# Feed-forward weight blocks in divided units: the first sum of each unit made by an accumulating transfer instead of VectorE

## The chip, the cores and the metric

The kernel runs on one core of one Trainium2 chip. A core has TensorE (PE, matrix products into PSUM), VectorE (DVE), ScalarE (ACT), GpSimd (POOL) and SyncE (SP), each with a queue of its own that it works through in order, and 16 DMA engines that all queues share. The metric is device time in microseconds (us), the median of several executions.

## What is computed

One inference step of a small hybrid decoder layer for 1048 tokens (16 meta tokens, 1024 prompt tokens, 8 single-token samples), model width 1024, in float32:

```python
def swiglu(x, wg, wu, wd):
    return (jax.nn.silu(x @ wg) * (x @ wu)) @ wd

def decoder_layer(h, ...):
    h = h + 0.5 * swiglu(rmsnorm(h, n1), w1g, w1u, w1d)
    u = rmsnorm(h, nm) @ w_in
    ...
    h = h + mix
    h = h + 0.5 * swiglu(rmsnorm(h, n2), w2g, w2u, w2d)
    return h, s_hg, s_ssm, conv_buf
```

Between the two feed-forward blocks lie two scans (an HGRN2 group and a Mamba-2 group) and an output projection. The change touches the two feed-forward blocks alone, and in them the products of the normed tokens with `wg` and `wu`. Hidden width is 2816, that is 22 columns of 128.

## The kernel before

**Products in three parts.** A float32 operand is split into a high and a low half in a faster format; a product is then three matmuls (high x high, high x low, low x high; lines 169 to 171). For a block of weights the high half is a cast on ScalarE (`hi`, line 497) and the low half a subtraction on VectorE (`lo`, line 501).

**Seven products for eight.** For one column of 128 hidden features, gate and up weights are cut along the model width into four blocks of 512 x 128, each stored on chip as 128 x 512. They are named by number: 1 (gate, first half), 7 (up, first half), 4 (up, second half) and 2 (gate, second half). A scheme of the Strassen kind replaces the eight block products with seven, at the price of sums of weight blocks, made in `Left.sum_`:

- 5 = 7 + 4
- 6 = 5 - 1
- 7 = 1 - 7, written over block 7
- 3 = 2 - 6

One column handled like this is a unit, a `Left` object. The sums are VectorE instructions over 128 x 512 (line 493).

**Divided units.** In each of the two feed-forward blocks the last 18 of the 22 columns are handled two at a time by `two_pairs`: product 3 of the two units is not done for each, but divided once more into seven smaller products for both together. These are the 18 divided units of a block, 36 in all. A pair of units takes 24 steps; a step is one product of 12 matmuls, in some steps with a smaller one behind it.

**What sets the order.** In the feed-forward blocks the queues of PE, VectorE, ScalarE and SP are written out by hand. `Steps` holds the PE steps; `S.before(i, fn)` puts a piece of other work ahead of step `i` in the program, and each engine's queue receives its instructions in that order. For a divided unit that begins at step `s0`, `plan_apart` (line 517) places loads at -10 to -7 (`load`, line 487, on SP's queue), sums at -5 to -2, and the split of each block 4 and 3 steps ahead of its product. POOL's queue is not written by hand; the scheduler places its instructions by what they depend on.

**Buffers.** Loaded blocks and sums lie in a ring of eight buffers of 128 x 512 (`raw`, tile name `r`). A load into a buffer waits on SP's queue until the buffer's last reader is done, and what stands behind it on SP waits too: also the stores of finished hidden blocks (line 994, `hd<-s`).

Of the kernel before, what the change touches and what calls it, by code (L numbers as in the profile page):

```python
# [13 lines left out]
ALU = mybir.AluOpType  # L14
# [3 lines left out]
P = 128  # L18
# [324 lines left out]
class Blocks:  # L343
# [19 lines left out]
    def sum_(self, p):  # L363
        x, y = {5: (7, 1), 6: (3, 5), 7: (3, 7), 4: (2, 6)}[p]
        x, y = self.b[x], self.b[y]
        t = self.b[p] if p == 7 else self.new(p)
        self.K.nc.vector.tensor_sub(t, x, y)  # L367
# [108 lines left out]
class Left:  # L476
# [8 lines left out]
    def load(self, p):  # L485
        self.raw[p] = self.K.raw(self.n * P)
        self.K.nc.sync.dma_start(self.raw[p].rearrange("p (k c) -> p k c", k=self.n), self.srcs[p])

    def sum_(self, p):
        x, y, op = {5: (7, 4, ALU.add), 6: (5, 1, ALU.subtract), 7: (1, 7, ALU.subtract), 3: (2, 6, ALU.subtract)}[p]  # L490
        if p not in self.raw:
            self.raw[p] = (self.K.t if p in self.apart else self.K.raw)(self.n * P)
        self.K.nc.vector.tensor_tensor(self.raw[p], self.raw[x], self.raw[y], op)  # L493
# [23 lines left out]
    def plan_apart(self, S, s0, uses):  # L517
        for p, d in ((7, -10), (4, -9), (1, -9), (2, -7)):
            S.before(s0 + d, lambda p=p: self.load(p))
        for p, d in ((5, -5), (6, -4), (7, -3), (3, -2)):  # L520
            S.before(s0 + d, lambda p=p: self.sum_(p))
        for p, d in uses.items():
            S.before(s0 + d - 4, lambda p=p: self.hi(p))
            S.before(s0 + d - 3, lambda p=p: self.lo(p))
# [515 lines left out]
def down(K, S, wdv, hidden, src, h, after):  # L1040
# [25 lines left out]
    def pieces(p, j, g, b, tag, late=0):  # L1066
# [33 lines left out]
        if p in (5, 6, 7, 3):  # L1100
            x, y = {5: (21, 22), 6: (0, 11), 7: (22, 0), 3: (12, 0)}[p]
            S.before(b - 9, lambda: sum_(x, y, ALU.add if p == 5 else ALU.subtract))
# [1465 lines left out]
```

## Time and profile before

| | us |
|---|---|
| median of 3 runs | 1922.8 (1922.28 to 1923.09) |
| the profiled execution | 1922.67 |
| its span | 1920.9 |

The profile is one execution seen by the hardware profiler. Its times count from the start of the span. Busy time of an engine is given in us, with the number of instructions in brackets where a window is shown; a row of a timeline has start, duration, engine, line, operation, output and inputs with the buffer numbers left out, and in square brackets the idle time before it and what ended it. A row for SP (SPq) is the issue of a transfer, not the transfer: what moves is seen in the last two columns of a window, the mean busy share of the 16 DMA engines and GB/s.

### The profile page before, as it was taken

The page shows a single profiled execution, that of the slowest core. Times are in us where ns is not written, and L with a number is a line of the kernel's source. Part 1 is how long each engine was busy: PE and PEld are TensorE (multiplying, and loading weights), DVE is VectorE, ACT ScalarE, POOL GpSimd, SP SyncE. Part 2 cuts the span into 40 slices and gives each one's busy share as a digit, 9 for nine tenths or more (in the row PEclk, how much of TensorE's full clock was granted, in tenths as well). Part 3 has the DMA queues.
Part 4 walks back from the last instruction along what each step waited for, and adds up shares of the span by engine and source line. Part 5 has one row for each costly group of instructions (what it writes and reads, how often), then busy time and mean ns, then how long its engine had stood idle before and what let it go on. Part 6 is the DMA issues. An engine that isn't in the chain of part 4 may idle for free.

```text
span 1920.9 us, 41195 instructions
## 1 busy us (share of the span) xinstructions
PE 1905.5 (99%) x16692; PEld 1875.2 (98%) x16692; DVE 1526.5 (79%) x2866; ACT 858.0 (45%) x1635; POOL 30.1 (2%) x88
## 2 busy tenths in 40 slices
PE   9999999999999999999999999999999999999998
PEld 9999999999999999999999999999999999999998
DVE  7888888889788877566585557999888888978974
ACT  6533333334534644466564545743333332453353
POOL 3000000000000000000000000000000000000000
PEclk9999999999999999999999999999999999999999
DMA  7143333335967541221463254133333333596852
GB/s 249 50 128 95 95 107 112 92 98 175 305 215 243 165 152 52 66 89 38 116 186 85 83 173 144 58 114 107 99 93 101 101 112 93 173 269 210 281 175 84
DMA packets 324209, 258.46 MB, mean 135 GB/s; under 512 B 18923, under 2 KB 298731, under 8 KB 324011
## 3 DMA queue, kind: packets, MB, share of 16 engines
q1 hardware_dynamic: 323779, 255.79, 43.1%
q8 instruction: 131, 2.15, 0.5%
q14 instruction: 59, 0.48, 0.1%
q0 software_dynamic: 224, 0.04, 0.0%
q10 hardware_dynamic: 16, 0.00, 0.0%
HBM read 190.79 MB, written 65.05 MB: 133 GB/s over the span
## 4 chain that ended last, share of the span: by engine, by line
PE 94%; DVE 3%; ACT 1%; issue 1%; DMA 0%; SPq 0%; DVEq 0%; ACTq 0%
PE acc L169 24%; PE acc L171 23%; PE acc L170 23%; PE mis L169 5%; PE mis L170 5%; PE mis L171 5%; PE mis L1963 1%; DVE u L382 1%; DVE u L367 1%; PE mis L1665 0%; PE mis L2030 0%; PE mis L1659 0%; DMA s<-in_x_prompt_dram 0%; PE mis L2055 0%; PE mis L1654 0%
## 5 line engine op out<-in xcount | busy, mean ns | idle before, releaser
L169 PE MATMUL acc<-u,ws 128*128 128x258 f32 (+4 forms) x3634 | 1064.0, 293 | 1.1 <-DVE u L1279 0.8
L171 PE MATMUL acc<-u,ws 128*128 128x258 f32 (+4 forms) x3634 | 1055.3, 290 | 0.7 <-DVE ws L501 0.7
L170 PE MATMUL acc<-u,ws 128*128 128x258 f32 (+4 forms) x3634 | 1054.8, 290 | 0.0
L169 PEld LDWEIGHTS acc<-u,ws 128*128 128x128 f32 x3634 | 686.5, 189 | 8.7 <-issue 6.2
L170 PEld LDWEIGHTS acc<-u,ws 128*128 128x128 f32 x3634 | 688.3, 189 | 0.8 <-DVE u L330 0.2
L171 PEld LDWEIGHTS acc<-u,ws 128*128 128x128 f32 x3634 | 686.1, 189 | 1.6 <-DVE ws L501 1.1
L169 PE MATMUL mis<-u,ws 128*128 128x262 f32 (+1 forms) x810 | 230.2, 284 | 0.0
L171 PE MATMUL mis<-u,ws 128*128 128x262 f32 (+1 forms) x810 | 228.7, 282 | 0.0
L170 PE MATMUL mis<-u,ws 128*128 128x262 f32 (+1 forms) x738 | 208.6, 283 | 0.0
L501 DVE TENSOR_TENSOR ws<-r,ws 128x512 fp32r<-128x512 f32 x266 | 181.6, 684 | 4.1 <-ACT ws L497 3.9
L901 ACT ACTIVATE t<-t 128x524 f32<-128x524 f32 (+1 forms) x72 | 46.1, 640 | 300.1 <-DVE t L898 300.1
L497 ACT CAST ws<-r 128x512 fp32r<-128x512 f32 x266 | 156.8, 615 | 42.2 <-PE mis L171 18.1
L169 PEld LDWEIGHTS mis<-u,ws 128*128 128x128 f32 x810 | 152.9, 189 | 0.1
L171 PEld LDWEIGHTS mis<-u,ws 128*128 128x128 f32 x810 | 152.7, 189 | 0.0
L170 PEld LDWEIGHTS mis<-u,ws 128*128 128x128 f32 x738 | 139.9, 190 | 0.1
L493 DVE TENSOR_TENSOR r<-r,r 128x512 f32<-128x512 f32 x150 | 100.8, 684 | 0.3
L1031 DVE TENSOR_TENSOR u<-u,u 128x1048 fp32r<-128x1048 f32 (+3 forms) x84 | 96.1, 1146 | 4.8 <-ACT u L1027 4.3
L1089 ACT CAST ws<-u 128x512 fp32r<-128x512 f32 (+1 forms) x72 | 42.1, 585 | 109.9 <-DVE u L1084 105.2
L164 DVE TENSOR_TENSOR ws<-r,ws 128x512 fp32r<-128x512 f32 x88 | 59.5, 685 | 38.3 <-ACT ws L163 38.0
L1027 ACT CAST u<-u 128x1048 fp32r<-128x1048 f32 (+3 forms) x84 | 82.8, 988 | 1.3 <-DMA u<-hd 1.3
L1118 DVE SCALAR_TENSOR_TENSOR s<-acc,s 128x524 f32<-128x524 f32 (+3 forms) x86 | 53.9, 651 | 35.3 <-PE acc L171 35.0
L898 DVE TENSOR_TENSOR t<-t,u 128x524 f32<-128x524 f32 (+1 forms) x108 | 73.2, 692 | 0.1
(465 smaller groups left out, 2329.1 us busy)
## 6 DMA issues: line engine op xcount, KB each, us to landing
r<-in_w_ffn_down_dram SPq DMA_DIRECT2D x128, 256.0 KB
hd<-s SPq DMA_DIRECT2D x93, 258.0 KB
r<-in_w_ffn_gate_dram SPq DMA_DIRECT2D x88, 256.0 KB
r<-in_w_ffn_up_dram SPq DMA_DIRECT2D x88, 256.0 KB
hd<-s SPq DMA_DIRECT2D x77, 262.0 KB
u<-hd SPq DMA_DIRECT2D x36, 516.0 KB
u<-hd SPq DMA_DIRECT2D x28, 524.0 KB
r<-in_w_in_dram SPq DMA_DIRECT2D x56, 256.0 KB
```

Of the source, the lines that this page charges most:

```text
L164: self.nc.vector.tensor_sub(lo, src, hi.bitcast(F32))
L169: mm(ps, whi, xhi, start=first, stop=False, skip_group_check=more)
L170: mm(ps, whi, xlo, start=False, stop=False, skip_group_check=more)
L171: mm(ps, wlo, xhi, start=False, stop=last, skip_group_check=more)
L493: self.K.nc.vector.tensor_tensor(self.raw[p], self.raw[x], self.raw[y], op)
L497: self.K.nc.scalar.copy(self.w[p][:, : self.n * P], self.raw[p])
L501: self.K.nc.vector.tensor_sub(t[:, 512 : 512 + w], self.raw[p], t[:, :w].bitcast(F32))
L898: nc.vector.tensor_mul(t, t if src is None else src, spread.lanes(n, slice(0, 2)))
L901: nc.scalar.activation(t, t, AF.Silu)
L1027: K.nc.scalar.copy(hi, lo.bitcast(F32))
L1031: K.nc.vector.tensor_sub(lo, lo.bitcast(F32), hi.bitcast(F32))
L1118: nc.vector.scalar_tensor_tensor(t, b, 0.5, t, ALU.mult, ALU.add)
```

## The change

```diff
+    def first_of(self, p):
+        self.raw[p] = self.K.raw(self.n * P)
+        self.K.nc.sync.dma_start(self.raw[p].rearrange("p (k c) -> p k c", k=self.n), self.srcs[7])
+
+    def second_of(self, p):
+        self.K.nc.gpsimd.dma_start(self.raw[p], self.raw[4], accum_op=ALU.add)
+
...
     def plan_apart(self, S, s0, uses):
         for p, d in ((7, -10), (4, -9), (1, -9), (2, -7)):
             S.before(s0 + d, lambda p=p: self.load(p))
-        for p, d in ((5, -5), (6, -4), (7, -3), (3, -2)):
+        S.before(s0 - 8, lambda: self.first_of(5))
+        S.before(s0 - 7, lambda: self.second_of(5))
+        for p, d in ((7, -4), (6, -3), (3, -2)):
             S.before(s0 + d, lambda p=p: self.sum_(p))
```

In each divided unit, block 5 = 7 + 4 is no longer made by VectorE. Block 7 is loaded from DRAM a second time, into the buffer of block 5 (`first_of`, step -8, SP's queue), and a transfer issued from POOL's queue reads block 4 from its buffer and adds it into block 5's (`second_of`, step -7). Sum 7 moves from step -3 to -4, and sum 6 from -4 to -3. The other units (`plan`) keep their VectorE sums.

SP's queue in the second divided unit of the first block; 7 is `r_216`, 4 is `r_219`, 1 is `r_220`, 2 is `r_224` before and `r_225` now, and 5 is `r_223` now. Before:

```order
L994 DMA hd_5_112<-s_208_1409 256x1x262
L487 DMA r_216_1482<-in_w_ffn1_up_dram 128x4x128
L487 DMA r_219_1500<-in_w_ffn1_up_dram 128x4x128
L487 DMA r_220_1502<-in_w_ffn1_gate_dram 128x4x128
L994 DMA hd_4_111<-s_218_1497 256x1x262
L994 DMA hd_7_114<-s_218_1497 256x1x262
L487 DMA r_224_1539<-in_w_ffn1_gate_dram 128x4x128
```

Now:

```order
L1003 DMA hd_5_112<-s_208_1410 256x1x262
L487 DMA r_216_1483<-in_w_ffn1_up_dram 128x4x128
L487 DMA r_219_1501<-in_w_ffn1_up_dram 128x4x128
L487 DMA r_220_1503<-in_w_ffn1_gate_dram 128x4x128
L1003 DMA hd_4_111<-s_218_1498 256x1x262
L491 DMA r_223_1524<-in_w_ffn1_up_dram 128x4x128
L1003 DMA hd_7_114<-s_218_1498 256x1x262
L487 DMA r_225_1542<-in_w_ffn1_gate_dram 128x4x128
```

The new load stands behind the first of two stores and ahead of the load of block 2.

VectorE's queue at the sums of the same unit; 6 is `r_229` before and `r_231` now, 3 is `r_234`, and before 5 is `r_227`. Before:

```order
L493 TENSOR_TENSOR r_227_1572<-r_216_1482,r_219_1500 128x512
L898 TENSOR_TENSOR t_228_1586<-acc_217_1484,u_144_888 128x524
L493 TENSOR_TENSOR r_229_1589<-r_227_1572,r_220_1502 128x512
L493 TENSOR_TENSOR r_216_1482<-r_220_1502,r_216_1482 128x512
L501 TENSOR_TENSOR ws_230_1591<-r_220_1502,ws_230_1591 128x512
L917 TENSOR_TENSOR t_232_1621<-acc_231_1593,t_221_1516 128x524
L991 TENSOR_TENSOR s_226_1569<-s_218_1497,s_208_1409 128x524
L493 TENSOR_TENSOR r_234_1626<-r_224_1539,r_229_1589 128x512
```

Now:

```order
L907 TENSOR_TENSOR t_228_1588<-acc_217_1485,u_144_888 128x524
L500 TENSOR_TENSOR r_216_1483<-r_220_1503,r_216_1483 128x512
L500 TENSOR_TENSOR r_231_1608<-r_223_1524,r_220_1503 128x512
L508 TENSOR_TENSOR ws_229_1592<-r_220_1503,ws_229_1592 128x512
L926 TENSOR_TENSOR t_232_1623<-acc_230_1594,t_221_1517 128x524
L1000 TENSOR_TENSOR s_227_1573<-s_218_1498,s_208_1410 128x524
L500 TENSOR_TENSOR r_234_1628<-r_225_1542,r_231_1608 128x512
```

Sum 5 is gone, sum 7 stands ahead of sum 6, and sum 6 reads the buffer that the transfer fills; behind it in the queue stand a split, a PSUM evacuation and sum 3.

POOL's queue, where the transfers of the first block begin:

```order
L1279 AFFINE_SELECT mf_1155_8935<-mf_1155_8935 128x64
L1282 CAST mask16_8938<-mf_1155_8935 32x16 x4
L494 DMA r_195_1302<-r_191_1280 128x512
L494 DMA r_223_1524<-r_219_1501 128x512
L494 DMA r_255_1764<-r_249_1732 128x512
```

They stand behind the masks that POOL builds at the start of the program; the 18 of the second block follow POOL's work for the scans.

## The prediction

> **What bounds the kernel now.** I read the page first, then busy time by stage, then the chain of waits inside the two stages that the change touches.
>
> ```profile
> span 1920.9 us, 41195 instructions
> PE 1905.5 (99%) x16692; PEld 1875.2 (98%) x16692; DVE 1526.5 (79%) x2866; ACT 858.0 (45%) x1635; POOL 30.1 (2%) x88
> PE 94%; DVE 3%; ACT 1%; issue 1%; DMA 0%; SPq 0%; DVEq 0%; ACTq 0%
> ...
> core 0: us, PE busy (x) PEld busy (x) DVE busy (x) ACT busy (x) POOL busy (x), PEclk, DMA share, GB/s
> 90.00:455.00 365.00, 364.84 (x2996) 364.43 (x2996) 320.23 (x575) 120.21 (x223) 0.00 (x0) 1.00 0.35 106
> 1308.00:1655.00 347.00, 347.00 (x2895) 347.00 (x2894) 304.10 (x549) 114.92 (x214) 0.00 (x0) 1.00 0.34 102
> 1429.60:1469.20 39.60, 39.60 (x333) 39.60 (x332) 34.55 (x63) 12.85 (x24) 0.00 (x0) 1.00 0.34 101
> ```
>
> The two rows that begin at 90 and 1308 us are the divided stages of the two feed-forward blocks, where the 36 changed units lie (18 in each block). PE is busy 364.84 of 365.00 us and 347.00 of 347.00, at a granted clock of 1.00. The last row is one pair of units, 39.60 us for 24 steps, so 1.65 us a step. VectorE is at 34.55 of 39.60 there: busy, but not what ends. So work taken from VectorE can give back at most the 0.16 us that PE stands still in those windows. A wait that the change adds costs only as far as it reaches PE.
>
> **What is removed.** The first sum of each unit was one VectorE instruction:
>
> ```profile
> L493 DVE TENSOR_TENSOR r<-r,r x150: 678/684/693, 66.7 to 1654.7; 128x512 f32<-128x512 f32 x150
> 122.03 1.28 DVE L493 TENSOR_TENSOR r<-r,r 128x512 f32<-128x512 f32 x2
> ```
>
> Two in a row take 1.28 us, so one more costs about 0.60 us of VectorE's queue. 36 times 0.60 is 21.6 us of VectorE, all of it beside a full PE: worth 0 to 0.16 us.
>
> **What is added.** Each unit gets a second load of block 7 on SP (256 KB) and a 256 KB transfer on the Pool queue that adds block 4 to it. SP had the time, and the windows show the DMA engines at 0.34 to 0.35. Per pair of units that is two more loads and two accumulating transfers. At 1.05 us for one pass of 256 KB over the engines (next rows), and three passes for an accumulating one, it is 8.4 us in 39.6, a share of 0.21: about 0.55 in all, so bandwidth does not bind. POOL had nothing to do in these windows, and what stands behind the transfers in its queue belongs to later stages. Block 5's buffer is held from step -8 instead of -5, so SP may find a buffer later; block 2, loaded behind it, is not needed until step -2.
>
> What can cost is the new wait. VectorE's sum 6 (block 5 minus block 1), at step -3, now waits for load 7, then the transfer, to land. Behind sum 6 in VectorE's queue stand the split of block 1, an evacuation of a PSUM bank, and sum 3; ScalarE's cast of sum 6 waits too, and through these PE. Let L be the time from the moment both inputs are there until the transfer has landed.
>
> **L, from the nearest rows.** A plain load when nothing else moves, and the only transfers that Pool issues before:
>
> ```profile
> 1401.90 0.37 SPq L487 DMA_DIRECT2D r<-in_w_ffn_gate_dram  x1
> 1403.00:1403.50 0.50, 0.50 (x6) 0.50 (x6) 0.41 (x1) 0.50 (x2) 0.00 (x0) 1.00 0.52 146
> 1403.50:1404.00 0.50, 0.50 (x6) 0.50 (x5) 0.48 (x1) 0.16 (x1) 0.00 (x0) 1.00 1.01 304
> 1404.00:1404.50 0.50, 0.50 (x7) 0.50 (x6) 0.50 (x2) 0.00 (x0) 0.00 (x0) 1.00 0.20 58
> ...
> L1234 POOL DMA_DIRECT2D t<-in_norm_mix_dram x1: 723/723/723, 1.4 to 1.4; - x1
> DMA to landing us min/median/max: 3.8/6.2/7.0
> ```
>
> The load is issued at 1401.90, its bytes move from about 1403.2 and end at about 1404.2: 2.3 us, of it some 1.05 us of moving. Pool's own transfers took 3.8 to 7.0 us to land, though they carry a few KB, from DRAM and beside the 512 KB input loads. An accumulating transfer reads two blocks and writes one; I count two more passes than the load has, 2.3 + 2 x 1.05 = **4.4 us**, an estimate between the two rows. Bounds: below, 2.3 us (the passes overlap); above, 7.0 us plus two passes, 9.1 us.
>
> The Trainium skill's "DMA: Bandwidth & Descriptors", section "Anatomy of one DMA — SWDGE (gpsimd) path", fits a Pool transfer as about 2.0 us plus its bytes at 436 GB/s, an estimate of 2.6 us here for a plain copy. By it next to nothing would wait and the sum would be 1922.7. This trace's landings of 3.8 us and more for a few KB stand against it.
>
> **Time there is for it, unit by unit.** The steady units have enough:
>
> ```profile
> 1424.75 0.37 SPq L487 DMA_DIRECT2D r<-in_w_ffn_gate_dram  x1
> 1437.42 0.68 DVE L493 TENSOR_TENSOR r<-r,r 128x512 f32<-128x512 f32 x1
> ...
> 1445.64 0.52 SPq L994 DMA_DIRECT2D hd<-s  x1
> 1454.39 1.29 DVE L493 TENSOR_TENSOR r<-r,r 128x512 f32<-128x512 f32 x2
> ```
>
> The new load stands just ahead of block 2's (1424.75) in a first unit of a pair, and ahead of the store at 1445.64 in a second. Landed 2.3 us later, at 1427.1 and 1447.9, it leaves 10.3 us and 6.5 us until sum 6, which takes the place of today's sum 7 (1437.42; second of two at 1454.39, so 1455.0, less the freed 0.6). 4.4 us is hidden in all 32 of them.
>
> The four units where the divided stages begin have less, since their loads come late and in a crowd. First unit, first block; then its second unit:
>
> ```profile
> 98.31 0.55 SPq L487 DMA_DIRECT2D r<-in_w_ffn_gate_dram  x1
> 98.00:102.00 4.00, 4.00 (x35) 4.00 (x35) 4.00 (x7) 1.62 (x3) 0.00 (x0) 1.00 1.04 311
> 102.00:103.00 1.00, 1.00 (x11) 1.00 (x10) 0.95 (x3) 1.00 (x3) 0.00 (x0) 1.00 0.24 76
> 105.84 0.69 DVE L493 TENSOR_TENSOR r<-r,r 128x512 f32<-128x512 f32 x1
> ...
> 115.92 2.35 SPq L994 DMA_DIRECT2D hd<-s  x2
> 117.00:118.00 1.00, 1.00 (x11) 1.00 (x10) 0.96 (x3) 0.00 (x0) 0.00 (x0) 1.00 0.76 268
> 119.00:122.00 3.00, 3.00 (x27) 3.00 (x26) 3.00 (x6) 0.00 (x0) 0.00 (x0) 1.00 1.00 305
> ```
>
> In the first, the new load takes the place of block 2's (98.31) in a queue that empties at 102.2 with one more transfer behind it, so it lands near 101.2; sum 6 is due at 105.84 - 0.6 = 105.2: 4.0 us. In the second it follows the store of 115.92, whose bytes end at 118.0, and lands near 119.1; sum 6 is due at 122.6 - 0.6 = 122.0: 2.9 us, with engines full from 119 to 122, so I add one pass, L = 5.45.
>
> The same two places in the second block:
>
> ```profile
> 1309.76 1.01 SPq L487 DMA_DIRECT2D r<-in_w_ffn_gate_dram  x2
> 1313.00:1314.00 1.00, 1.00 (x11) 1.00 (x10) 0.76 (x2) 0.63 (x1) 0.00 (x0) 1.00 0.64 184
> 1319.54 0.69 DVE L493 TENSOR_TENSOR r<-r,r 128x512 f32<-128x512 f32 x1
> ...
> 1329.66 2.33 SPq L994 DMA_DIRECT2D hd<-s  x2
> 1331.00:1332.00 1.00, 1.00 (x11) 1.00 (x10) 0.97 (x2) 0.00 (x0) 0.00 (x0) 1.00 0.63 218
> 1335.72 1.28 DVE L493 TENSOR_TENSOR r<-r,r 128x512 f32<-128x512 f32 x2
> ```
>
> Landed near 1313.6 and due at 1318.9: 5.3 us. Landed near 1332.7 (the store's bytes end about 1331.6, then one load) and due at 1335.7: 3.0 us, L again 5.45.
>
> VectorE therefore waits 0.4, 2.55, 0 and 2.45 us. What of it reaches PE depends on VectorE's own idle time around these places:
>
> ```profile
> 99.00:127.00 28.00, 27.84 (x227) 27.47 (x226) 27.19 (x46) 10.44 (x19) 0.00 (x0) 1.00 0.43 130
> 1308.00:1340.00 32.00, 32.00 (x269) 32.00 (x269) 29.58 (x48) 12.02 (x22) 0.00 (x0) 1.00 0.39 116
> ```
>
> In the first block VectorE has 0.8 us to spare and PE already dips; in the second 2.4 us. So PE loses 0.4 + 2.55 - 0.8 = 2.15 us and 2.45 - 2.4 = 0.05 us. Sum: **+2.2 us**. The profiled execution's own time is 1922.67 us (span 1920.9 and 1.8 around it), against a median of 1922.8: 1922.67 + 2.2 = **1924.9 us**. About 0.2%, 3.8 us, is what a measurement here tells from no change, so this is "the same".
>
> **Rivals.**
>
> *All hidden.* L is 3 us or less, near a plain load. At 3.0 the waits are 0, 1.15, 0 and 1.05 us, and 1.15 - 0.8 = 0.35 is left; below 2.65 nothing is: 1922.8. For it, the load's 2.3 us; against it, Pool's landings.
>
> *Slower: the transfer takes as long as Pool's transfers did.* L = 6.5, between their median and longest. Waits 2.5, 4.65, 1.2, 4.55, less the covers 0.8 and 2.4: +9.7, 1932.4. It decides from L of about 5. For it, the landing row; against it, those landings ran beside the input loads. The 16 steady second units still hide it, 6.5 against 6.5.
>
> *Slower: Pool can write the transfer only in VectorE's gaps.* VectorE is idle 5.05 of 39.60 us, so an issue of 0.6 us (0.72 in the row) would stretch to 4.7, L = 8.5 to 9. At 9.0 the four waits are 5.0, 7.15, 3.7 and 7.05 us, less 3.2: +19.7, 1942.4. The steady second units would wait 2.5 us, still inside the 5.05 us of idle; further on the waits run into the next pair and tens of us follow. No row shows Pool issuing under a busy VectorE, which is why it keeps a chance. The Trainium skill's "SBUF — State Buffer", section "Who interferes with whom", has VectorE shut Pool out in its two-port modes, and says that a tensor_tensor has none; the groups of VectorE in these stages are nearly all TENSOR_TENSOR, so by that page this does not happen.
>
> *Faster.* Needs 3.8 us from stages where PE stands 0.16 us. That the change does not do what it says is excluded: the instruction order has 36 sums fewer on VectorE and 36 transfers more on Pool.
>
> **How the numbers follow.** Forecast (L from 3.0 to 4.9) 0.40, all hidden 0.14, as long as Pool's 0.28, in the gaps or beyond 0.16, faster 0.02. The same is 0.40 + 0.14 = 0.54, slower 0.28 + 0.16 = 0.44, faster 0.02. The forecast's own range is 1923.0 to 1926.5. The range runs from 1922.0, below which PE has nothing to give, to 1940, short of the case in the gaps: some 0.18 is left out.
>
> **What would show it.** L: on Pool, the accumulating transfers from issue to landing. The waits: VectorE idle before the two or four sums 6 near 105, 122, 1319 and 1336, released by a DMA, and none before the steady ones. PE: about 362.7 us of 365 busy in the first block's window, unchanged in the second. VectorE's busy time falls by 36 x 0.684 = 24.6 us, to about 1502, without any gain. Wrong would be waits of VectorE for a DMA in every pair of units, or PE idle where VectorE did not wait.

## The result and the profile after

| | median us (runs) | lowest to highest |
|---|---|---|
| before | 1922.32 (12) | 1920.6 to 1923.48 |
| after | 1925.88 (12) | 1923.92 to 1928.25 |

The ratio after to before is 1.002, 95% interval 1.0011 to 1.0029: 2.1 to 5.6 us slower. The middle of it, 0.2%, is just about the 3.8 us that the prediction put as the bound of "the same". The profiled execution of after took 1928.05 us (span 1926.3), near the upper end of its runs, so sums below are made from stalls inside the stages and not from the two spans.

The page of after, its span, busy times and chain of waits:

```profile
span 1926.3 us, 41373 instructions
PE 1907.9 (99%) x16692; PEld 1876.7 (97%) x16692; DVE 1507.2 (78%) x2830; ACT 858.0 (45%) x1635; POOL 63.5 (3%) x124
PE 91%; DVE 5%; ACT 1%; issue 1%; DMA 1%; SPq 0%; DVEq 0%; ACTq 0%
```

VectorE does 19.3 us less than before (1526.5), and the kernel is no faster for it. In the chain of waits VectorE has a larger share (5%, it was 3%) though it does less. The share says where to look and not how much is lost: 2% of the span would be some 39 us. The windows of the two divided stages of after, columns as before:

```profile
90.00:455.00 365.00, 363.19 (x2977) 362.17 (x2976) 310.20 (x555) 119.55 (x222) 15.51 (x18) 1.00 0.46 129
1308.00:1655.00 347.00, 345.90 (x2879) 345.30 (x2878) 292.69 (x528) 113.40 (x212) 15.38 (x18) 1.00 0.46 127
```

PE lacks 1.81 us in the first (0.16 before) and 1.10 in the second (0 before). DMA share rose from 0.35 and 0.34 to 0.46: far from full. Where PE lost them is in its timeline; these are all of PE's rows in the entry units that have idle time ahead of them:

```profile
109.00 0.36 PE L169 MATMUL acc<-u,ws 128*128 128x262 f32 x1 [1.21 <-DVE t L616]
127.59 0.39 PE L171 MATMUL acc<-u,ws 128*128 128x262 f32 x1 [0.23 <-DVE ws L508]
130.76 0.36 PE L169 MATMUL mis<-u,ws 128*128 128x262 f32 x1 [0.24 <-DVE t L928]
...
1344.79 0.39 PE L171 MATMUL acc<-u,ws 128*128 128x258 f32 x1 [0.82 <-DVE ws L508]
1347.95 0.36 PE L169 MATMUL mis<-u,ws 128*128 128x258 f32 x1 [0.26 <-DVE t L928]
```

Together 2.76 us, inside the interval of 2.1 to 5.6. VectorE releases PE each time, with an evacuation (`t`) or a split (`ws`). One step back, VectorE's own timeline at sum 6 of the four entry units and of one steady unit (the last row):

```profile
106.95 0.69 DVE L500 TENSOR_TENSOR r<-r,r 128x512 f32<-128x512 f32 x1 [1.68 <-DMA r<-r]
...
126.24 0.69 DVE L500 TENSOR_TENSOR r<-r,r 128x512 f32<-128x512 f32 x1 [3.02 <-issue]
...
1323.13 0.68 DVE L500 TENSOR_TENSOR r<-r,r 128x512 f32<-128x512 f32 x1
...
1343.44 0.69 DVE L500 TENSOR_TENSOR r<-r,r 128x512 f32<-128x512 f32 x1 [4.06 <-issue]
...
1363.94 0.68 DVE L500 TENSOR_TENSOR r<-r,r 128x512 f32<-128x512 f32 x1
```

Three waits of 1.68, 3.02 and 4.06 us. The first names the transfer (`DMA r<-r`); the other two say "issue", which means only that the profile shows no releaser, and the experiments below settle that it is the same transfer. And one step further back, Pool's timeline: when it begins to issue each transfer, which I read as the moment when both inputs are there (four entry units, then a steady one):

```profile
103.60 0.94 POOL L494 DMA_DIRECT2D r<-r  x1 [81.92 <-DMA r<-in_w_ffn_gate_dram]
121.53 0.86 POOL L494 DMA_DIRECT2D r<-r  x1 [16.99 <-DVE s L1000]
...
1319.75 0.86 POOL L494 DMA_DIRECT2D r<-r  x1 [216.40 <-DVE s L768]
1337.57 0.85 POOL L494 DMA_DIRECT2D r<-r  x1 [16.96 <-DVE s L1000]
1355.76 0.85 POOL L494 DMA_DIRECT2D r<-r  x1 [17.34 <-DMA r<-in_w_ffn_gate_dram]
```

The releasers that the profile names in these rows, a VectorE instruction (`s`) or a load of gate weights, are no inputs of the transfer (blocks 7 and 4 are up weights), so the reading rests on the fourth experiment: there the second load of block 7 moves ahead in the entry units, and the transfer begins earlier with it, by 0.9 to 4.3 us against sum 7 of the same unit.

From 1337.57 to sum 6 at 1343.44 are 5.87 us; from 1355.76 to 1363.94 8.2 us, in which the transfer is long done. The group of all 36:

```profile
L494 POOL DMA_DIRECT2D r<-r x36: 847/854/937, 103.6 to 1651.5; - x36
DMA to landing us min/median/max: 3.2/3.6/5.8
```

Long landings are not a matter of the entry units alone: the steady transfers that begin at 298.11, 418.82 and 1552.62 take 5.2, 5.6 and 5.5 us, and the time until sum 6 hides them. What sets the three waiting units apart is how late their transfers begin: 1.7 to 1.8 us before VectorE is ready for sum 6, less than the shortest landing of 3.2.

Last, a steady pair. The instruction that stands once in each pair on VectorE's queue (`t<-r,t`, 128 x 256), two in a row, of before and then of after:

```profile
166.71 0.42 DVE L804 TENSOR_TENSOR t<-r,t 128x256 f32<-128x256 f32 x1
206.86 0.42 DVE L804 TENSOR_TENSOR t<-r,t 128x256 f32<-128x256 f32 x1
```

```profile
168.82 0.42 DVE L813 TENSOR_TENSOR t<-r,t 128x256 f32<-128x256 f32 x1
208.97 0.42 DVE L813 TENSOR_TENSOR t<-r,t 128x256 f32<-128x256 f32 x1
```

40.15 us apart in both kernels (39.6 in the second block, in both). A mark like this is a better measure of a steady stage than PE's busy share: it cannot be blurred by modelled ends of matmuls. (In the run with two transfers below, the interval from 219.03 to 259.59 has PE busy for all of its 40.56 us, and is 0.41 us longer than here all the same.) The steady pairs gain and lose nothing.

### The profile page after: what moved, and what is told of

Its sections match the earlier page's. It is cut to its first block, busy times and chain, and to the rows that moved or that the text cites. A ratio compares the mean times of both kernels' runs of the same rounds, so it can differ in the third digit from the quotient of the medians.

```text
span 1926.3 us, 41373 instructions
## 1 busy us (share of the span) xinstructions
PE 1907.9 (99%) x16692; PEld 1876.7 (97%) x16692; DVE 1507.2 (78%) x2830; ACT 858.0 (45%) x1635; POOL 63.5 (3%) x124
## 3 DMA queue, kind: packets, MB, share of 16 engines
q0 software_dynamic: 5408, 9.48, 2.8%
q8 instruction: 131, 2.15, 0.5%
## 4 chain that ended last, share of the span: by engine, by line
PE 91%; DVE 5%; ACT 1%; issue 1%; DMA 1%; SPq 0%; DVEq 0%; ACTq 0%
PE acc L169 23%; PE acc L171 22%; PE acc L170 22%; PE mis L169 5%; PE mis L171 5%; PE mis L170 5%; PE mis L1972 1%; DVE u L382 1%; DVE ws L508 1%; DVE u L367 1%; PE mis L1674 1%; PE mis L2039 0%; PE mis L1668 0%; DMA s<-in_x_prompt_dram 0%; PE mis L2064 0%
## 5 line engine op out<-in xcount | busy, mean ns | idle before, releaser
L500 DVE TENSOR_TENSOR r<-r,r 128x512 f32<-128x512 f32 x114 | 76.3, 683 | 8.9 <-issue 7.1
L824 ACT CAST ws<-t 128x512 fp32r<-128x512 f32 (+1 forms) x54 | 29.6, 548 | 98.0 <-DVE t L813 57.0
```

## The experiments

The theory to test: the time is lost only where the divided stages begin, since there the transfer is issued too late for sum 6; the 32 steady units hide it. Rivals: a small loss spread over all 36 units; the second load of block 7 (SP's queue, buffers) as the cause and not the transfer; the length of the transfer itself.

**Entry units back on VectorE.** `entry` is true for the first pair of a block.

```diff
+        if entry:
+            for p, d in ((5, -5), (6, -4), (7, -3), (3, -2)):
+                S.before(s0 + d, lambda p=p: self.sum_(p))
+        else:
...
```

> Only the first pair of divided units in each feed-forward block makes its first sum on VectorE again; the other 32 units keep the accumulating transfer. Entry theory (the whole loss is VectorE's wait in the units where a divided stage begins): PE is full in both divided stages as before (0.2 us lost or less), time 1922 to 1923, ratio to before 0.9995 to 1.0005. Spread theory (the transfers cost a little in every unit, by sharing DMA engines or ports): 32/36 of the change's +3.6 us stays, about 1925.5.

1921.85 us, ratio 0.9997 (0.9988 to 1.0005). The windows:

```profile
90.00:455.00 365.00, 364.84 (x2997) 364.41 (x2996) 312.88 (x559) 120.25 (x223) 13.80 (x16) 1.00 0.46 129
1308.00:1655.00 347.00, 347.00 (x2895) 347.00 (x2894) 296.34 (x534) 114.65 (x214) 13.70 (x16) 1.00 0.46 126
```

PE is full as before the change, with 32 transfers (16 + 16 on POOL) still in place. So the four entry units carry the whole loss.

**Only the entry units.** The same with `if not entry:`: 4 transfers, 32 units summed on VectorE.

> The opposite half: only the four entry units use the accumulating transfer, the 32 others sum on VectorE. Entry theory: the full loss is there, about 1925 to 1926, with VectorE waiting about 1.7, 3.0 and 4 us in three of the four units and PE standing about 2.7 us. Spread theory: 4/36 of +3.6 us, so 1922.7.

1926.23 us, ratio 1.0021 (1.0012 to 1.003).

```profile
90.00:455.00 365.00, 363.08 (x2975) 362.05 (x2974) 317.03 (x570) 118.95 (x221) 1.80 (x2) 1.00 0.35 106
1308.00:1655.00 347.00, 345.80 (x2878) 345.20 (x2878) 300.44 (x543) 111.96 (x209) 1.73 (x2) 1.00 0.35 103
```

PE lacks 1.92 and 1.20 us: four transfers cost what 36 cost. The two runs together exclude a loss spread over the units.

**The load kept, the sum on VectorE.** All 36 units load block 7 a second time, and VectorE adds block 4 to it in place.

```diff
-        S.before(s0 - 7, lambda: self.second_of(5))
+        S.before(s0 - 5, lambda: self.K.nc.vector.tensor_add(self.raw[5], self.raw[5], self.raw[4]))
```

> All 36 units load block 7 a second time as in the change, but VectorE adds block 4 into that buffer at step -5; no accumulating transfer. Entry theory (the wait is for the transfer, not for the second load): 1922 to 1923.5. Rival (the second load itself, its place on SP's queue and its 9.4 MB, is what comes late): 1924.5 to 1926.

1922.25 us, ratio 1.0001 (0.9992 to 1.001); PE 364.40 of 365.00 and 347.00 of 347.00, one stall of 0.49 us in the first entry unit. The load itself costs next to nothing; the transfer does.

**The load earlier in the entry units.** There, the second load of block 7 stands right behind the load of block 4; all 36 transfers are kept.

```diff
-        for p, d in ((7, -10), (4, -9), (1, -9), (2, -7)):
+        for p, d in ((7, -10), (4, -9), *(((5, -9),) if entry else ()), (1, -9), *(() if entry else ((5, -8),)), (2, -7)):
...
```

> The change, but in the four entry units the second load of block 7 is issued directly behind block 4's load, ahead of block 1's and of the stores. Entry theory: the transfer starts 1 to 6 us earlier there, VectorE's waits go to under 1 us each, PE loses 0 to 1 us, time 1922.0 to 1923.5. If the transfer's own length or a cost in all units decides, the time stays at 1925 to 1926.

1920.83 us, ratio 0.9996 (0.9987 to 1.0005). Pool's row at the place that had the longest wait; then VectorE's rows, first the one wait that is left, then the same place:

```profile
1329.99 0.85 POOL L494 DMA_DIRECT2D r<-r  x1 [13.56 <-DVE s L629]
```

```profile
107.60 0.69 DVE L500 TENSOR_TENSOR r<-r,r 128x512 f32<-128x512 f32 x1 [0.99 <-DMA r<-r]
...
1335.45 1.28 DVE L500 TENSOR_TENSOR r<-r,r 128x512 f32<-128x512 f32 x2
```

With the transfer begun at 1329.99, 5.5 us ahead of the sums, sums 7 and 6 run as one pair (1.28 us for two) without a wait; in the second unit of the first block they do the same (begun at 118.44, sums at 123.19). What is left is one PE stall of 0.52 us in the first entry unit (PE 364.36 of 365.00 and 347.00 of 347.00). The loss cannot be told any more; the median lies 1.2 us under the 1922.0 that I had as the lower end, but against the kernel before there is no gain that these runs can tell, as expected with PE full.

**The transfer twice.** Issued two times, the second behind the first; block 4 is then added twice, so the products of block 5 are changed.

```diff
-        self.K.nc.gpsimd.dma_start(self.raw[p], self.raw[4], accum_op=ALU.add)
+        for _ in range(2):
+            self.K.nc.gpsimd.dma_start(self.raw[p], self.raw[4], accum_op=ALU.add)
```

> All 36 divided units; the accumulating transfer is issued twice, the second behind the first, so block 4 is added twice into block 5 (the computation is changed there). It doubles the suspected cost L. If the time is lost only in the entry units, and the steady units hide a transfer for as long as their slack (6.3 us and more) and after that for as long as VectorE's idle time (5.05 us a pair): L about 7 us in the steady units, waits there under 1 us in second units only, PE not touched by them; the four entry waits grow by some 3.5 us each, to about 5, 6.5, 2 and 7.5 us, PE loses 8 to 14 us, all of it before 150 us and between 1308 and 1360, time 1930 to 1937. If every unit pays for part of its transfer, the loss is 36 times whatever the second transfer adds: 1950 and more, spread evenly. If the transfers overlap or the wait is not what costs: 1926.

1954.78 us, ratio 1.0171 (1.0158 to 1.0185): more than the 1930 to 1937 of my theory, and the number given to the rival, though not in its manner: by the once-per-pair marks the two entries take 22 us of it and the 14 steady intervals 10.3 (second mark of the first block at 178.91 us where it was at 166.71, the last at 464.60 for 447.73; in the second block 1406.82 for 1380.09 and 1689.52 for 1657.19). Two reasons. First, the steady units: L was 8.3 us in a second unit, not 7 (166.36 to 174.63). Pool's timeline there, then VectorE's in both units of the pair:

```profile
166.36 0.87 POOL L495 DMA_DIRECT2D r<-r  x1 [15.06 <-DVE t L908]
170.54 0.86 POOL L495 DMA_DIRECT2D r<-r  x1 [3.30 <-DMA r<-r]
```

```profile
155.60 0.69 DVE L501 TENSOR_TENSOR r<-r,r 128x512 f32<-128x512 f32 x1 [0.37 <-DMA r<-r]
174.63 0.69 DVE L501 TENSOR_TENSOR r<-r,r 128x512 f32<-128x512 f32 x1 [1.86 <-DMA r<-r]
```

Both units of a pair wait, and though the waits stay below VectorE's idle time of 5.05 us a pair, all but one of the 14 steady intervals are longer, by 0.26 to 2.28 us. Idle time elsewhere in the pair does not pay for a wait here. Second, the entries: VectorE waits 5.71, 6.39, 4.29 and 7.75 us there, where I had about 5, 6.5, 2 and 7.5, and PE's stalls behind these are 5.26, 2.99, 3.11 and 5.02 us, together 16.4 where I had 8 to 14. And a stall of PE can cost more than its length. After PE's 5.26 us of idle that end at 112.47:

```profile
113.00:114.00 1.00, 1.00 (x7) 1.00 (x6) 1.00 (x2) 0.00 (x0) 0.00 (x0) 0.50 0.00 0
...
116.00:117.00 1.00, 1.00 (x10) 1.00 (x9) 0.60 (x1) 0.98 (x2) 0.00 (x0) 1.00 0.98 276
```

The third column from the right, PEclk, is 0.50, and PE starts 7 matmuls in a microsecond where it starts 10 or 11 at 1.00. PE is "busy" all the time. More on this in the last section.

**The transfer three times.** `range(3)`; block 4 is added three times.

> As with the transfer issued twice, but three times in series: block 4 is added three times into block 5. L becomes some 10.5 us, beyond the slack of both steady units (8.2 and 6.3 us measured between Pool's issue and the sum). By the slack theory waits appear in every steady pair (2 to 4 us each unit) and with the entry's they pass VectorE's 5.05 us of idle a pair: PE loses 1 to 4 us in each of the 16 steady pairs, time 1955 to 1990, a break between two and three transfers that no straight line through one and two (2 to 12 us) gives. If the loss grows in a line with L in the entry units alone: 1938 to 1948, and PE full in the steady pairs.

2085.74 us, ratio 1.086 (1.0844 to 1.0877), beyond my 1990. From one to two transfers the time grows by 29 us, from two to three by 131: the break that the slack theory asks for, and no straight line. One steady pair, between its marks:

```profile
240.56:287.92 47.36, 43.01 (x332) 42.63 (x331) 33.71 (x62) 12.89 (x24) 5.14 (x6) 0.93 0.51 129
```

47.36 us in place of 40.15. PE is idle for 4.35 us of it, more than the 1 to 4 that I gave; the other 2.9 us fit the clock, 0.93 in the mean, which I had not counted. Both together are why the size was missed.

**A plain copy.** The same transfer without the addition: block 5 becomes block 4, and block 7 is left out of it.

```diff
-        self.K.nc.gpsimd.dma_start(self.raw[p], self.raw[4], accum_op=ALU.add)
+        self.K.nc.gpsimd.dma_start(self.raw[p], self.raw[4])
```

> All 36 units; the same transfer from Pool's queue as a plain copy, so block 5 becomes block 4 and block 7 is left out of it. It measures what the addition itself costs in L. If the transfer's length goes by passes over the engines (an accumulating one reads two blocks and writes one, a copy reads one and writes one): landing about 1 us less, 2.3 to 2.6 us minimum and median instead of 3.2 and 3.6; the entry waits each about 1 us shorter, PE loses about 1 us instead of 2.75, time 1923 to 1924.5. If the addition costs nothing and the length is that of Pool's queue and the route: landing 3.2 and 3.6, time 1926.

1923.56 us, ratio 1.0008 (0.9999 to 1.0017); PE 364.36 of 365.00 and 346.66 of 347.00.

```profile
L494 POOL DMA_DIRECT2D r<-r x36: 538/538/637, 103.4 to 1648.1; - x36
...
DMA to landing us min/median/max: 2.2/2.8/5.0
```

The copy lands 1.0 us earlier at the least and 0.8 at the median, and 0.3 of that is Pool's issue (538 ns, not 854). So the addition costs about 1 us of L. It does not explain the longest landings: the copy's own, 5.0 us, is at the same place as the change's 5.8.

**Block 2's load later in the entry units.** To take it out of the transfer's way, from step -7 to -5.

```diff
-        for p, d in ((7, -10), (4, -9), (1, -9), (2, -7)):
+        for p, d in ((7, -10), (4, -9), (1, -9), (2, -5 if entry else -7)):
```

> The change with one difference: in the four entry units the load of block 2 stands at step -5 instead of -7, so that it doesn't move beside the transfer. If L in the second entry units (4.7 and 5.8 us against 3.3 elsewhere) comes from the crowd, in which one engine of the 16 ends last: L there 3.3 to 4 us, waits of VectorE at the second entry units about 1.5 to 2.2 instead of 3.0 and 4.1 us, no loss of PE in the second block (347.0 of 347) and about 1 us in the first, time 1922.5 to 1924, unless block 2 itself comes late: then a wait at sum 3, step -2, takes its place (VectorE released by a load of the gate weights). If L is long there for another reason (the stores on SP's queue, the buffers' places): L stays 4.7 and 5.8, time 1926.

1926.52 us, ratio 1.0024 (1.0014 to 1.0034): no help. It does not decide, because the edit did not do what it was for. SP's timeline of this kernel in the second entry unit of the second block:

```profile
1332.66 0.60 SPq L491 DMA_DIRECT2D r<-in_w_ffn_up_dram  x1
1333.90 1.25 SPq L1003 DMA_DIRECT2D hd<-s  x2
1335.24 0.57 SPq L487 DMA_DIRECT2D r<-in_w_ffn_gate_dram  x1
```

The load follows 2.6 us behind the new one (1.9 in the change: 1333.82 and 1335.68). SP's queue only keeps an order; a step number sets no time on it when SP has nothing to wait for. The load still moved beside the transfer, L was 5.4 us, and what makes L long there stays open. That L is 3.3 us elsewhere, as I had it, was wrong as well: the steady units have long landings too (above).

## Why the prediction was right, step by step

**What bounds: right.** PE full at a clock of 1.00, so that VectorE's freed time is worth nothing: the runs with 32 sums off VectorE (1921.85) and with none (1922.25) are the same. VectorE's busy time fell by 19.3 us and not by the 24.6 given: I took the 0.684 us of a group's row, where an instruction overlaps the one before it (1.28 for two). My own 0.60 for one would have given 21.6; the last 2.3 us were not traced. Nothing hung on it.

**Steady units hidden: right.** 40.15 us a pair in both kernels. Between Pool's issue and sum 6 there were at the least 8.2 us in a first and 6.3 us in a second unit, where I gave 10.3 and 6.5.

**Bandwidth: right.** 0.46, less than the 0.55 I allowed.

**The four entry units: right mechanism, three terms off, and they partly cancel.** That the total came within 0.6 us of the stalls found is in part luck. Slack is the time from Pool's issue until VectorE is ready for sum 6 (the start of its wait).

| unit | slack: predicted, measured | L: predicted, measured | wait: predicted, measured |
|---|---|---|---|
| first block, first | 4.0, 1.67 | 4.4, 3.35 | 0.4, 1.68 |
| first block, second | 2.9, 1.69 | 5.45, 4.71 | 2.55, 3.02 |
| second block, first | 5.3, 3.38 | 4.4, 3.3 | 0, 0 |
| second block, second | 3.0, 1.81 | 5.45, 5.87 | 2.45, 4.06 |

*The slack* was 1.2 to 2.3 us too long everywhere. I had the new load land 2.3 us behind its issue, or where the bytes ahead of it end. In SP's timeline of after it is issued at 98.27, 117.65 and 1333.82 in the three units that wait, and Pool starts 5.33, 3.88 and 3.75 us later. Here the second of them, and then the load and the Pool row of a steady unit, where the DMA engines stand still as the load is issued (share 0.00 from 1450 to 1451):

```profile
117.65 0.56 SPq L491 DMA_DIRECT2D r<-in_w_ffn_up_dram  x1
...
1450.12 0.37 SPq L491 DMA_DIRECT2D r<-in_w_ffn_up_dram  x1
1453.76 0.87 POOL L494 DMA_DIRECT2D r<-r  x1 [19.31 <-DVE t L930]
```

The steady unit takes 3.64 us, and the 32 steady units take 3.38 to 4.33. So the two second entry units are no exception, and the 2.3 us were too short everywhere: they ended with the load's bytes, and Pool starts more than a microsecond after that. Only the first entry unit of each block takes longer, 5.33 and 5.59 us. That this is mostly the load and not Pool is seen in the run with the sum on VectorE: there VectorE's add waits for a load of up weights in the first entry unit (0.55 us), and starts 5.12 us behind the issue of the second load of block 7 (97.77 to 102.89).

*L* was about 1 us too long in the uncrowded units. I had counted two whole extra passes of 1.05 us for the addition; the copy against the accumulating transfer shows about 1.0 us in all. The sentence on the Trainium skill's "DMA: Bandwidth & Descriptors", section "Anatomy of one DMA — SWDGE (gpsimd) path", deserved more weight: its 2.6 us for a plain copy lies between the copy's 2.2 and 2.8 here. The 3.8 us and more of Pool's transfers at the start, which I held against it, were the poorer witness. The time that I worked out by that sentence, 1922.7 with next to no wait, did not come all the same: with the slack of under 2 us even the copy was waited for, 0.70, 2.83 and 3.31 us. Only in the last unit was L longer than I gave, 5.87.

*The covers* I took as one sum per block, 0.8 and 2.4 us of VectorE's idle time in a window. They belong to a place. Wait of VectorE and PE's stall behind it at the first entry unit, from five kernels (copy, early load, the change, only the entry units, block 2 later): 0.70 and 0.24, 0.99 and 0.52, 1.68 and 1.21, 1.81 and 1.35, 1.84 and 1.39. The difference is 0.45 to 0.47 each time. At the second unit it is 2.55 to 2.6 (3.02 and 0.47, 3.03 and 0.43, 2.82 and 0.24), and in the second block 2.94 to 3.07 (4.06 and 1.08, 4.11 and 1.17, 3.68 and 0.72, 3.31 and 0.24). So PE's loss is a wait less a fixed cover, 0.46, 2.57 and 2.97 us: 1.22 + 0.45 + 0 + 1.09 = 2.76, which is what PE's rows sum to (the covers are fitted to these kernels, so the sum only shows that they agree). I had 2.15 + 0.05 + 0 = 2.2. The second block's loss, which I put at nearly nothing ("unchanged", and PE has 345.90 of 347.00), came from a wait of 4.06 where I had 2.45.

**The rivals.** *All hidden* fell: three waits are there. *As long as Pool's early transfers* fell as a rule (median 3.6, not 6.5), though the last entry unit came near it. *Only in VectorE's gaps* fell: Pool issues in 847 to 937 ns beside a VectorE that is busy 85% of these windows, and the copy in 538 to 637, where Pool's transfers at the program's start take 518 to 723. The Trainium skill's "SBUF — State Buffer", section "Who interferes with whom", had it so for tensor_tensor, and the trace agrees. *Faster* fell.

**What stays open.** The median rose by 3.6 us and the stalls found are 2.76; the interval (2.1 to 5.6) holds both, so the remainder is not shown to be anything. And what makes some landings long, as said; and what lies between the last bytes of a load and the start of who waits for it.

## What to carry to other kernels

Work that was moved off an engine with idle time gained nothing here, since another engine was full; it could only cost, and it cost at the places where the new wait has little slack, which here was the first pair of each stage and not the 32 units of the steady run. Cost such a wait place by place: moment when the inputs are there, duration, moment when it is needed, and the cover at that very place; and take the duration of a transfer from its issue to the start of an instruction that waits for it, not to the end of its bytes. If the move is wanted for other reasons, issue its inputs earlier in the first iterations alone, as the fourth experiment did.

## What the runs showed of the hardware

**An accumulating transfer against a copy.** The rows of the transfer queue that Pool's transfers use (packets, MB, share of 16 engines' span), of before, of after and of the copy:

```profile
q0 software_dynamic: 224, 0.04, 0.0%
```

```profile
q0 software_dynamic: 5408, 9.48, 2.8%
```

```profile
q0 software_dynamic: 3104, 9.48, 1.3%
```

For the same 256 KB an accumulating transfer has (5408 - 224) / 36 = 144 packets and a copy 80, and its packets take 2.8 / 1.3, some 2.2 times as long: 1.5 us of all 16 engines each, against 0.7.

**A tail on few engines.** Windows of after around the longest landing (transfer issued at 1337.57, sum 6 at 1343.44; the next-to-last column is the DMA share):

```profile
1339.00:1340.00 1.00, 1.00 (x11) 1.00 (x10) 0.39 (x1) 1.00 (x3) 0.00 (x0) 1.00 1.21 314
1340.00:1341.00 1.00, 1.00 (x10) 1.00 (x10) 0.00 (x0) 1.00 (x2) 0.00 (x0) 1.00 0.96 176
1341.00:1342.00 1.00, 1.00 (x10) 1.00 (x9) 0.00 (x0) 0.00 (x1) 0.00 (x0) 1.00 0.15 28
1342.00:1343.00 1.00, 1.00 (x11) 1.00 (x10) 0.00 (x0) 0.00 (x0) 0.00 (x0) 1.00 0.06 13
```

For over a microsecond 0.06 of the engines, one of 16, still moves while VectorE waits (its column is 0.00). In the copy the place is long too (5.0 us), and with the earlier load, which moves the transfer away from it, L is 3.8. What that one engine has in front of it was not found.

**The price of a PE stall.** In the change's stalls, up to 1.21 us, the granted clock stays at 1.00. The run with two transfers has five stalls of over 1 us, and length alone does not decide there. Those of 1.42 and 3.11 us leave the clock at 1.00; that of 2.99 us does not. PE's row and a window behind it, for 2.99 and for 3.11:

```profile
134.98 0.39 PE L171 MATMUL acc<-u,ws 128*128 128x262 f32 x1 [2.99 <-DVE ws L509]
137.00:138.00 1.00, 1.00 (x7) 1.00 (x6) 0.96 (x4) 0.00 (x0) 0.00 (x0) 0.50 0.62 204
...
1339.18 0.36 PE L169 MATMUL acc<-u,ws 128*128 128x258 f32 x1 [3.11 <-DVE t L617]
1340.00:1341.00 1.00, 1.00 (x11) 1.00 (x10) 1.00 (x3) 0.00 (x0) 0.00 (x0) 1.00 0.00 0
```

The clock is at 0.50 for 3.4 us behind the stall of 2.99; for 6.8 us around that of 5.26, 3.5 of them behind it; and for 6.8 us around that of 5.02, 6.2 of them behind it. The Trainium skill's "TensorE: Matmul & The Clock Gate", "Part 1: The HAM clock gate", puts it at half rate after an idle window of about 3.4 us and back after as long a busy one. The lengths agree, once 3.4 us and two times twice that; but 2.99 us of idle were already enough here. So where the clock fell, a stall cost 1.7 to 3.1 us (half of 3.4 to 6.2) beyond its own length, and PE's busy share does not show that: read the clock column too.
